# Gated DeltaNet layer on one core: the planner's periods replaced by five chains

## The chip, the cores and the metric

One core of one Trainium2 chip. The metric is device microseconds (us) of one execution of the whole program, the median of several runs. Engines are called as in the profile: PE (matmul; PEld is its weight load), DVE, ACT, POOL, SP (which issues DMAs). Each engine runs its own list of instructions in order and waits on semaphores for the others.

## The reference, cut to what matters

One layer (DEPTH = 1), so the attention mixer of the reference is never reached. x is 1024 x 1024.

```python
h    = rms_norm(x) * (1 + scale(c)) + shift(c)
proj = h @ w_in                      # 8 heads of q, of k; 16 of v, of z; b, a
qkv  = silu(causal_conv4(qkv))       # depthwise, 4 taps
q, k = l2norm(q) * 128**-0.5, l2norm(k)
beta, g = sigmoid(b), -exp(a_log) * softplus(a + dt_bias); gc = cumsum(g) by chunk of 64
decay = exp(where(lower, gc[c] - gc[s], -inf))
t    = inverse(I + strict_lower(beta k k^T * decay))
# scan over chunks
v_new = t(beta v) - t(beta k exp(gc)) @ state
o     = (q exp(gc)) @ state + (q k^T * decay) @ v_new
state = state * exp(gc_last) + (k exp(gc_last - gc))^T @ v_new
out   = rms_norm(x + gate(c) * ((rms_norm(o) * silu(z)) @ w_out))
```

## The kernel before

**Numbers.** All is f32. The large products run as three fp32r matmuls: every factor is split into a high half (`whi`, written by ACT, L586) and a low half (`wlo`, written by POOL, L587), and hi*hi, hi*lo and lo*hi are added in PSUM. A "tile" is 128 output columns of `w_in` against all 1024 tokens: 2 halves of 24 matmuls of 512 columns (`project`, L598).

**Groups.** The 16 v heads are worked on in 8 groups of two, with their common q and k head. For group gi:

- `proj_kq`: tiles of k and q, each with a convolution (`Conv`: ACT copies, three DVE operations L557, a Silu on ACT L561).
- `norms`: loads the decay exponents `em` (128 x 2048), 16 DVE additions (L641), one Exp on ACT (L644); k and q are transposed on PE (L659, L667) and their norms taken.
- `stage_a`: per chunk a product of k with k and q (L704), DVE makes `at` from it (L706); then by DRAM to another layout, 31 steps of substitution on DVE (L733, L736, one after the other), back by DRAM, and two calls of `levels` (L766 to L800), which build the inverse `TT` of each half of the tokens on PE, DVE and ACT.
- `values`: two v tiles with convolution, then a turn on PE (L813).
- `out_gate`: one z tile; its Silu (L868) is stored to DRAM.
- `scan`: 8 steps, each ks (L940), r on DVE (L943), ts (L963), vd on DVE (L967), vh and o on ACT (L969, L975), oq (L973, and in `second` L910), state (L982, L987). `second` of a step is issued in the next one. Outputs that are ready wait in a list `late`; `finish` turns one (L892), scales it (L896) and multiplies it by z (L897).

`residual_gate` makes the layer's gate (DVE at lowest rank), `early_loads` and `early` begin the output projection (L1067) with 4 of its 16 heads as soon as the projections are over.

**Who sets the order.** Between 78 us and about 1000 us the order on every engine is written out by a planner that runs while the kernel is built. Each stage is a generator; it issues a PE instruction and advances a clock `order.now`, puts other engines' operations into queues with an estimated cost, and yields a condition. An operation starts in the model when its inputs are ready (`LAT` after them, and no earlier than `now + LAT` of its issue); among operations that are ready on an engine the lowest `rank` goes first. `done` is true `LATP` after the modelled end. `drive` steps, at each turn, the first stage in its list whose condition holds. The chip then runs these orders with semaphores: where the model was wrong, an engine stands at the head of its list and waits.

`drive` is called once per **period** gi = -1 .. 7, and returns when all stages of that period are over:

```python
streams.append(scan(gi, Gs[gi]))
streams.append(stage_a(gi + 1, Gs[gi + 1], ...))
more = proj_kq(gi + 2, Gs[gi + 2], ...)
filler = [zfill, values(gi + 1, Gs[gi + 1], more)]
must = [Run(g) for g in streams] + [Run(itertools.chain(*filler))]
drive(background + must + ([zruns[gi + 2]] if ...) + [trun] * (gi >= HQ - 2), must)
```

So a period holds the scan of one group, `stage_a` (with `norms` in it) of the next and the k and q tiles of the one after; the z tiles of the following period (`zruns[gi + 2]`) can be taken early. In groups 0 and 7 the second `levels` call stands beside the scan (`LEV1`). The output projection's other 12 heads follow outside the planner.

## Time and profile before

| | |
|---|---|
| median of 3 runs | 1152.65 us (1149.68 to 1159.56) |
| profiled execution | 1154.56 us, its span 1152.8 us |
| granted TensorE clock, mean | 0.97 |
| busy: PE, PEld, DVE, ACT, POOL | 1075.8, 859.8, 757.8, 542.7, 440.1 us |

The span is first to last instruction. A matmul's row lasts longer than the step to the next one, since matmuls are pipelined; so PE's busy time is no measure of its work, but the time in which PE is *not* busy is time in which nothing flowed through it. Idle time stands before an instruction with what ended it.

### The profile page before, as it was taken

To read this page: it belongs to the slowest core of one execution; us is meant where nothing else is said; L and a number is where in the kernel's file an instruction comes from. 1 tells how busy PE (TensorE), PEld (TensorE's weight loads), DVE (VectorE), ACT (ScalarE), POOL (GpSimd) and SP (SyncE) were. 2 spreads that over 40 slices of the span, in tenths; PEclk is the share of its full clock that TensorE was granted. 3 is DMA by queue.
4 is the path that set the end of the run, shared out by engine and by line. 5 is a ranking of instruction groups with operands and counts; after the bars stand their busy time and mean duration, and the time that the engine had idled before them with its cause. 6 is when DMAs were issued, how large, how long until landed. Compare 5 with 4: busy or idle time off the path is not lost.

```text
span 1152.8 us, 18300 instructions
## 1 busy us (share of the span) xinstructions
PE 1075.8 (93%) x6295; PEld 859.8 (75%) x6295; DVE 757.8 (66%) x1913; ACT 542.7 (47%) x1415; POOL 440.1 (38%) x530
## 2 busy tenths in 40 slices
PE   7999998989999999899989998999999889999997
PEld 7877786867787777677867786778787657788785
DVE  5458963697789757776686678577767766413514
ACT  6457921443662346336623743374356424424523
POOL 3351321352352115313622452154215234844643
PEclk9899997999999889999999999999999979999999
DMA  9812142233154322421423052215212474335441
GB/s 286 224 37 91 42 119 69 69 102 95 40 150 120 84 78 67 122 69 47 119 61 110 27 148 56 75 39 144 65 56 70 115 231 134 101 114 182 153 128 73
DMA packets 187555, 118.43 MB, mean 103 GB/s; under 512 B 59669, under 2 KB 166470, under 8 KB 186438
## 3 DMA queue, kind: packets, MB, share of 16 engines
q1 hardware_dynamic: 186960, 117.15, 35.7%
q8 instruction: 50, 0.82, 0.3%
q14 instruction: 43, 0.35, 0.1%
q10 hardware_dynamic: 502, 0.10, 0.0%
HBM read 91.98 MB, written 25.24 MB: 102 GB/s over the span
## 4 chain that ended last, share of the span: by engine, by line
PE 43%; DVE 23%; ACT 11%; DMA 8%; issue 6%; POOL 6%; SPq 2%; DVEq 0%; ACTq 0%; POOLq 0%
PE pj L598 20%; DVE tm L733 5%; DVE tb L736 5%; PE pj L1067 4%; DVE vT L557 3%; DMA ua<-D 2%; DVE em L641 2%; DMA woraw<-in_gdn_w_out 2%; POOL wolo L206 2%; PE tr L704 2%; PE tr L797 2%; PE tr L789 2%; ACT tr L662 1%; ACT tr L669 1%; DVE kq L557 1%
## 5 line engine op out<-in xcount | busy, mean ns | idle before, releaser
L587 POOL TENSOR_TENSOR wlo<-wraw,whi 128x512 fp32r<-128x512 f32 x88 | 120.1, 1380 | 301.0 <-ACT whi L586 291.3
L733 DVE TENSOR_TENSOR tm<-tb,ua 128x126 f32<-128x126 f32 (+22 forms) x248 | 81.2, 327 | 25.3 <-DMA ua<-D 18.9
L557 DVE SCALAR_TENSOR_TENSOR kq<-xb,taps,kq 128x512 f32<-128x512 f32 x96 | 76.4, 804 | 22.3 <-ACT kq L554 19.2
L736 DVE TENSOR_TENSOR tb<-tb,tm 128x126 f32<-128x126 f32 (+22 forms) x248 | 82.2, 331 | 6.9
L557 DVE SCALAR_TENSOR_TENSOR vT<-xb,taps,vT 128x512 f32<-128x512 f32 x96 | 82.1, 855 | 5.0 <-ACT vT L554 3.9
L598 PE MATMUL pj<-h0hia,whi 128*128 128x512 f32 x184 | 77.6, 422 | 1.3 <-ACT kq L554 1.3
L598 PE MATMUL pj<-h0loa,whi 128*128 128x512 f32 x184 | 78.6, 427 | 0.0
L598 PE MATMUL pj<-h1lob,whi 128*128 128x512 f32 x184 | 77.4, 421 | 0.0
L598 PE MATMUL pj<-h0hia,wlo 128*128 128x512 f32 x184 | 77.2, 419 | 0.0
L598 PE MATMUL pj<-h0lob,whi 128*128 128x512 f32 x184 | 76.7, 417 | 0.0
L598 PE MATMUL pj<-h1loa,whi 128*128 128x512 f32 x184 | 76.3, 414 | 0.0
L598 PE MATMUL pj<-h1hia,wlo 128*128 128x512 f32 x184 | 76.2, 414 | 0.0
L598 PE MATMUL pj<-h0hib,wlo 128*128 128x512 f32 x184 | 76.0, 413 | 0.0
L598 PE MATMUL pj<-h1hia,whi 128*128 128x512 f32 x184 | 75.3, 409 | 0.0
L598 PE MATMUL pj<-h1hib,whi 128*128 128x512 f32 x184 | 75.3, 409 | 0.0
L598 PE MATMUL pj<-h0hib,whi 128*128 128x512 f32 x184 | 74.7, 406 | 0.0
L598 PE MATMUL pj<-h1hib,wlo 128*128 128x512 f32 x184 | 74.6, 405 | 0.0
L922 POOL TENSOR_TENSOR sso<-sso,neg_half 128x2 f32<-128x2 f32 x64 | 45.6, 713 | 71.4 <-DVE sso L920 67.9
L552 ACT COPY xb<-pj 128x512 f32<-128x512 f32 x62 | 36.1, 582 | 67.4 <-PE pj L598 63.7
L897 POOL TENSOR_TENSOR oT<-oT,z 128x256 f32<-128x256 f32 x64 | 48.1, 751 | 51.7 <-ACT oT L896 44.9
L896 ACT ACTIVATE oT<-pot,cols 128x256 f32<-128x256 f32 x64 | 30.3, 474 | 78.5 <-PE pot L892 76.8
L206 POOL TENSOR_TENSOR wolo<-woraw,wohi 128x512 fp32r<-128x512 f32 x36 | 48.7, 1371 | 44.7 <-ACT wohi L205 44.7
(459 smaller groups left out, 2923.6 us busy)
## 6 DMA issues: line engine op xcount, KB each, us to landing
wraw<-in_gdn_w_in SPq DMA_DIRECT2D x92, 256.0 KB, 3.3
woraw<-in_gdn_w_out SPq DMA_DIRECT2D x50, 256.0 KB, 3.2
wa<-in_ada_w SPq DMA_DIRECT2D x16, 512.0 KB, 7.0
em<-gc_dram SPq DMA_DIRECT2D x8, 1024.0 KB, 5.3
z_dram<-sz SPq DMA_DIRECT2D x32, 256.0 KB, 2.1
z<-z_dram SPq DMA_DIRECT2D x64, 128.0 KB, 2.4
o_dram<-oT SPq DMA_DIRECT2D x64, 128.0 KB, 1.9
gsrc<-o_dram SPq DMA_DIRECT2D x32, 256.0 KB, 3.0
```

The source lines that it names most:

```text
L206: nc.gpsimd.tensor_tensor(lo, raw, hi.bitcast(F32), op=ALU.subtract)
L552: a = act(lambda: nc.scalar.copy(xb[:, NTAP - 1:], ps), 512, *old, rank=0, holds=held)
L557: d = [vec(lambda j=j: nc.vector.scalar_tensor_tensor(dst, xb[:, j:j + TH], tp[:, j], dst, op0=ALU.mult, op1=ALU.add), 512, *d)]
L587: ops.append(pool(lambda raw=raw, ks=ks, hi=hi, lo=lo: nc.gpsimd.tensor_tensor(lo[:, ks], raw, hi[:, ks].bitcast(F32), op=ALU.subtract), 1 ...
L598: nc.tensor.matmul(ps, lhsT=a[:, k], rhs=b[half][k // 4][:, k % 4], start=(k == 0 and n == 0), stop=(k == KT - 1 and n == 2))
L641: e = [vec(lambda n=n, h=h: nc.vector.scalar_tensor_tensor(em[:, h, n], em[:, h, n], ngc[:, n, h0 + h:h0 + h + 1], mask, op0=ALU.add, op1= ...
L733: d = [vec(lambda j=j, mm=mm, ln=ln, tmv=tmv: nc.vector.tensor_tensor(tmv, tb[:, :mm, j:j + 1].to_broadcast([P, mm, ln]), ua[:, j:j + 1, j ...
L736: d = [vec(lambda j=j, mm=mm, tmv=tmv: nc.vector.tensor_tensor(tb[:, :mm, j + 1:], tb[:, :mm, j + 1:], tmv, op=ALU.subtract), 220 + mm * l ...
L896: a = act(lambda: nc.scalar.mul(oT, pot, normw_c), 470, holds=held)
L897: b = pool(lambda: nc.gpsimd.tensor_tensor(oT, oT, z, op=ALU.mult), 800, a, zo)
L922: d = pool(lambda: nc.gpsimd.tensor_tensor(sso, sso, neg_half[:, :2], op=ALU.pow), 700, d)
L1067: nc.tensor.matmul(acc, lhsT=a[:, ts], rhs=b, start=(first and n == 0), stop=(last and n == 2))
```

## The change

- The periods go. `drive` is called once, with five chains that each run over all 8 groups: scans; `outputs` (the former `finish`, now a stage of its own, with `late` and the fetched z tiles shared by all groups); `stage_a`, with both `levels` calls in it for every group; `norms`, one group after the other; and one chain of projections in the order values(0), z, values(1), k and q of 2, z, values(2), and so on. Beside them run the loader, the gate, and the early part of the output projection.
- What the periods had kept apart is now kept by conditions: buffers `kq`, `vtok`, `TT`, `em` wait for the scans that read them (`passed`, `gone`). `order.lock` and `LEV1` go.
- The PSUM bank `oq` is counted: a step of the scan is not issued before the planner thinks its readers done (`free("oq")`).
- The Exp over `em` is issued as four pieces of 128 x 512, at rank 2.
- `wlo` on POOL gets rank 2 and cost 1400 (was 1290).
- An operation is taken to start no earlier than `now + 380` after its issue (`LATE`; was 200), `LATP` is 300 (was 320).

```diff
-LATS, LAT, LATP, DMA = 50, 200, 320, 2800
+LATS, LAT, LATP, LATE = 50, 200, 300, 380
...
-        op = Op(eng, cost, fn, [a for a in after if a is not None], rank, table, self.now + LAT)
+        op = Op(eng, cost, fn, [a for a in after if a is not None], rank, table, self.now + LATE)
...
-                    lo[:, ks], raw, hi[:, ks].bitcast(F32), op=ALU.subtract), 1290, a, holds=r))
+                    lo[:, ks], raw, hi[:, ks].bitcast(F32), op=ALU.subtract), 1400, a, rank=2, holds=r))
...
+                    yield lambda: not old or done(old.passed[hf])
                     G.kq.append(cp.tile([P, 2, TH], F32, name="kq", tag="kq", bufs=4))
...
-        yield lambda: hasattr(order, "gate") and done(*order.gate, order.gc)
+        yield lambda: hasattr(order, "gate") and done(*order.gate, order.gc) and (gi < 2 or Gs[gi - 2].gone())
...
-        G.emop = act(lambda: nc.scalar.activation(em, em, AF.Exp), 1820, *e, table="exp")
+        G.emop = [[act(lambda x=em[:, h, n:n + 4]: nc.scalar.activation(x, x, AF.Exp), 512, *e[2 * n:2 * n + 8], rank=2,
+                       table="exp") for h in range(2)] for n in range(0, NT, 4)]
...
-        yield from levels(gi, G, 0, old)
-        if gi not in LEV1:
-            yield from levels(gi, G, 1, old)
+        yield from levels(gi, G, 0)
+        yield from levels(gi, G, 1)
...
-        yield lambda: not order.lock and (not (hf and old) or done(old.passed[0]))
-        order.lock = True
+        yield lambda: 2 * gi + hf < 3 or done(Gs[gi - 2 + hf].passed[1 - hf])
...
+                        yield lambda: 2 * gi + hf < 3 or done(Gs[gi - 2 + hf].passed[1 - hf])
                         G.vtok.append(cp.tile([P, 4, 2, P], F32, name="vtok", tag="vtok", bufs=3))
...
-                d = vec(lambda: nc.vector.tensor_tensor(o, o, po[:, 1], op=ALU.add), 256, *oo)
+                d = vec(lambda: nc.vector.tensor_tensor(o, o, po[:, 1], op=ALU.add), 256, *oo, holds=held)
...
-            yield lambda: hf in G.TTop and done(*ro, G.TTop[hf], G.nop[hf][4], *G.emop2)
+            yield lambda: hf in G.TTop and done(*ro, G.TTop[hf], G.nop[hf][4], *G.emop2) and free("oq")
             TT = G.TT[hf]
-            po = bank("oq", (P, 2, 2, P))
+            po, held = bank("oq", (P, 2, 2, P)), order.hold("oq", 3 if n else 1)
...
+        scans = Run(chain(scan(gi, G) for gi, G in enumerate(Gs)))
+        finishing, last = Run(outputs()), Run(early())
+        drive([Run(loader()), Run(early_loads()), Run(streams0), scans, finishing,
+               Run(chain(stage_a(gi, G) for gi, G in enumerate(Gs))), Run(chain(norms(gi, G) for gi, G in enumerate(Gs))),
+               Run(residual_gate()),
+               Run(chain([proj_kq(1, Gs[1])] + [values(gi, G, chain(others(gi))) for gi, G in enumerate(Gs)])), last],
+              [scans, finishing, last])
```

`others(gi)` yields `proj_kq(gi + 1)` (for gi > 0), then the z tiles: 5 after group 0, then 2, and 1 before the last.

## Rows read from the trace of the kernel before

**Rows 1.** The page: busy time and instructions of each engine.

```profile
PE 1075.8 (93%) x6295; PEld 859.8 (75%) x6295; DVE 757.8 (66%) x1913; ACT 542.7 (47%) x1415; POOL 440.1 (38%) x530
```

**Rows 2.** Windows by stage: start:end, length, busy us of each engine, PEclk, DMA.

```profile
76.00:181.00 105.00, 100.40 (x457) 80.00 (x456) 80.66 (x208) 61.42 (x143) 27.91 (x32) 1.00 0.24 74
181.00:202.00 21.00, 16.83 (x122) 12.55 (x121) 4.72 (x11) 2.70 (x5) 2.50 (x2) 0.61 0.33 78
202.00:297.00 95.00, 89.57 (x663) 71.22 (x663) 72.54 (x179) 39.27 (x108) 32.44 (x45) 1.00 0.33 88
297.00:421.00 124.00, 116.04 (x692) 91.57 (x690) 100.38 (x285) 57.15 (x157) 42.08 (x53) 0.96 0.36 98
...
638.00:747.00 109.00, 103.04 (x653) 82.48 (x652) 78.52 (x204) 53.92 (x153) 39.37 (x51) 1.00 0.30 81
...
919.00:961.00 42.00, 34.09 (x194) 24.00 (x193) 27.15 (x55) 10.92 (x19) 14.80 (x11) 0.80 0.61 191
961.00:1010.00 49.00, 47.07 (x321) 38.69 (x320) 26.83 (x65) 24.62 (x82) 34.27 (x41) 1.00 0.41 124
```

**Rows 3.** The same view, one window from 76 us to 1010 us.

```profile
76.00:1010.00 934.00, 873.83 (x5327) 694.93 (x5326) 670.23 (x1758) 448.14 (x1244) 335.84 (x427) 0.97 0.32 90
```

**Rows 4.** Windows with the projections' matmuls alone (L598): PE, PEld, PEclk, DMA.

```profile
638.00:747.00 109.00, 76.97 (x288) 52.70 (x288) 1.00 0.30 81
```

**Rows 5.** Chain that ended last, 266 to 273 us: start, us, what.

```profile
266.28 5.60 PE pj L598 x24
```

**Rows 6.** Waits of PE: who waited for whom, us in total, times, longest.

```profile
PE tr L813 <- ACT vT L561: 16.1, 11, 2.9
PE oq L973 <- DVE o L913: 7.7, 6, 1.6
PE ks L982 <- DVE vd L967: 6.9, 13, 1.1
...
PE tr L766 <- DVE TE L758: 3.5, 1, 3.5
PE ts L963 <- DVE r L943: 2.9, 6, 1.7
...
PE tr L778 <- ACT pn L772: 1.4, 1, 1.4
...
PE tr L789 <- DVE TE L782: 1.2, 1, 1.2
```

**Rows 7.** Timeline, all engines, 549 to 553 us: start, us, what, idle before.

```profile
547.89 1.28 ACT L644 ACT_TABLE_LOAD   x1
...
549.18 1.91 ACT L644 ACTIVATE em<-em 128x2048 f32<-128x2048 f32 x1
...
551.00 0.61 ACT L975 ACTIVATE o<-oq,eall 128x128 f32<-128x128 f32 x2
...
551.64 0.42 DVE L913 TENSOR_TENSOR o<-o,oq 128x256 f32<-128x256 f32 x1 [0.28 <-ACT o L975]
...
552.21 0.67 PE L973 MATMUL oq<-st,kq 128*128 128x256 f32 x2 [1.31 <-DVE o L913]
```

**Rows 8.** Timeline of DVE, then of PE, around 580 to 594 us.

```profile
581.32 0.30 DVE L733 TENSOR_TENSOR tm<-tb,ua 128x133 f32<-128x133 f32 x1
581.65 1.29 DVE L736 TENSOR_TENSOR tb<-tb,tm 128x133 f32<-128x133 f32 x1
...
589.98 0.74 DVE L557 SCALAR_TENSOR_TENSOR vT<-xb,taps,vT 128x512 f32<-128x512 f32 x1
...
593.11 0.66 PE L813 MATMUL tr<-ident,vT 128*128 128x128 f32 x4 [2.81 <-ACT vT L561]
```

**Rows 9.** Timeline: group 7's last k/q tile, first L704, first scan step.

```profile
856.53 0.69 ACT L554 ACTIVATE kq<-pj,taps 128x512 f32<-128x512 f32 x1
...
879.89 1.03 PE L704 MATMUL tr<-kq 128*128 128x256 f32 x4
...
960.87 0.61 PE L963 MATMUL ts<-vtok,TT 128*128 128x128 f32 x4
```

More of the change, by code (lines that the diff above doesn't have):

```diff
@@ L616, in __init__, with gone, proj_kq @@
             self.vop, self.ats, self.inverted = {}, None, [False, False]
-            self.nop, self.TTop = [], {}
-    def proj_kq(gi, G, old):
+            self.nop, self.TTop, self.normed, self.left = [], {}, False, None
+        def gone(self):
+            return self.left is not None and all(o.end is not None for o in self.left)
+    def proj_kq(gi, G):
         G.kq = []
+        old = Gs[gi - 2] if gi > 1 else None
         for j, ct in ((0, 8 + gi), (1, gi)):
@@ L868, in out_gate, with fetch @@
             load(store, act(lambda ps=ps, sz=sz: nc.scalar.activation(sz, ps, AF.Silu), 512, rank=0, table="silu",
-                            holds=ph))
+                            holds=ph), holds=held)
             yield None
+    late, zs = [], {}
+    def fetch():
+        for G, gi, n, *_ in late:
+            if (gi, n) not in zs and len(zs) < ZB and G.gated[n // 4] == 2:
+                z = cp.tile([P, 2, P], F32, name="z", tag="z", bufs=ZB)
+                zs[gi, n] = z, load(lambda z=z, n=n, h=2 * gi: nc.sync.dma_start(
+                    out=z, in_=z_dram[h:h + 2, :, n * P:(n + 1) * P].rearrange("h e t -> e h t")))
@@ new lines, in finish @@
+    def finish():
+        G, gi, n, o, op = late.pop(0)
+        pot, held = bank("pot", (P, 2, P)), order.hold("pot", 1)
+        for h in range(2):
+            nc.tensor.transpose(pot[:, h], o[:, h], ident)
+        order.now += M2
+        oT, stored = cp.tile([P, 2, P], F32, name="oT", tag="oT", bufs=OB), order.hold("oT", 1)
+        z, zo = zs.pop((gi, n))
+        a = act(lambda: nc.scalar.mul(oT, pot, normw_c), 470, holds=held)
+        b = pool(lambda: nc.gpsimd.tensor_tensor(oT, oT, z, op=ALU.mult), 800, a, zo)
+        load(lambda: nc.sync.dma_start(
+            out=o_dram[2 * gi:2 * gi + 2, :, n * P:(n + 1) * P].rearrange("h e t -> e h t"), in_=oT), b, holds=stored)
@@ L888, in finish @@
-        def finish():
-            n, o, op = late.pop(0)
-            pot, held = bank("pot", (P, 2, P)), order.hold("pot", 1)
-            for h in range(2):
-                nc.tensor.transpose(pot[:, h], o[:, h], ident)
-            order.now += M2
-            oT, stored = cp.tile([P, 2, P], F32, name="oT", tag="oT", bufs=OB), order.hold("oT", 1)
-            z, zo = zs.pop(n)
-            a = act(lambda: nc.scalar.mul(oT, pot, normw_c), 470, holds=held)
-            b = pool(lambda: nc.gpsimd.tensor_tensor(oT, oT, z, op=ALU.mult), 800, a, zo)
-            load(lambda: nc.sync.dma_start(
-                out=o_dram[h0:h0 + 2, :, n * P:(n + 1) * P].rearrange("h e t -> e h t"), in_=oT), b, holds=stored)
-            fetch()
@@ L902, in can_finish, with second @@
-        def can_finish():
-            fetch()
-            return late and late[0][0] in zs and done(late[0][2]) and free("pot") and order.avail("oT", OB)
-        def second(n, po, vh, vo, o, oo):
+        def second(n, po, vh, vo, o, oo, held):
             hf, j = divmod(n, 4)
@@ L946, in scan @@
                 second(*pend)
-                if len(late) > 2 and can_finish():
-                    finish()
                 if n < NT - 1:
@@ L988, in scan @@
                               rank=-1)
-            pend = (n, po, vh, vo, o, oo)
+            pend = (n, po, vh, vo, o, oo, held)
             yield lambda: done(*vo)
         second(*pend)
-        while late:
-            yield can_finish
-            finish()
+        G.left = [op for q in order.queue.values() for op in q]
+        yield None
     never = Op()
     def residual_gate():
+        yield lambda: Gs[RG - 1].left is not None
         gate_c = const.tile([P, KT], F32, name="gate_c")
@@ L1207, in drive @@
                 assert idle < 20000, [r.gen for r in must if not r.over]
-    def follow(run):
-        while not run.over:
-            yield lambda: run.over or not run.wait or run.wait()
-            run.step()
     order.projecting, order.early0 = True, False
```

100 lines of the change are left out of this document (35 added, 65 removed).

## The prediction, made before the changed kernel was run

> **What bounds the kernel now.** I read the page first: PE is busy for 1075.8 of 1152.8 us and no other engine is over 66% [rows 1]. PE's busy time overstates work, so I went on with what is left over: the time in which PE is not busy, stage by stage [rows 2], and over the whole stretch that the planner orders, 76 to 1010 us, in one row [rows 3]. The reader should see two things there. PE idles 934.0 - 873.8 = 60 us, and its clock is 0.97 of full speed on average, which is at most 0.03 x 934 = 28 us more. All other 846 us are matmuls that the change neither adds nor removes. So the most that any new order can win is 60 + 28 = 88 us, and this needs a perfect one.
>
> Next question: does PE idle because the periods leave it without work? I looked at a middle period, 638 to 747 us. It is 109 us long and PE is busy for 103.0 of it at full clock [rows 2]; it runs 288 projection matmuls, which is exactly the six tiles (two each of z, v and k/q, 48 matmuls each) that a period owes [rows 4]. A tile's half goes through in 5.60 us for 24, 233 ns each [rows 5], so projections take 288 x 0.233 = 67 us and the scan, products, turns and levels the rest. A join of periods would show as a hole of many us at 638 or 747; the whole period has 6 us, in pieces. So in the middle the joins cost next to nothing directly: z tiles of the next period fill them.
>
> What the idle time is made of stands in the table of PE's waits [rows 6]. Its longest single wait is 3.5 us. These are waits at the head of PE's list: the planner believed an operand finished that was not. The two largest kinds, with a picture each:
>
> - PE waits for DVE to empty the bank oq: 7.7 us in six waits. One of them in time order [rows 7]: the table load and the big Exp hold ACT for 1.28 + 1.91 us; the two small ACT operations on o start only at 551.00; DVE's addition follows at 551.64; then PE may write the bank, 1.31 us late.
> - PE waits for the Silu of vT before its turn: 16.1 us in eleven waits. DVE was in the substitution, one of whose operations had just taken 1.29 us in place of 0.30, and the convolution of vT began only at 589.98; the turn came 2.8 us late although other projections could have run [rows 8].
>
> At both ends it is worse: 181 to 202 us has 4.2 us idle and a clock of 0.61, 919 to 961 us has 7.9 us idle and a clock of 0.80 [rows 2].
>
> **The change part by part**, as PE time saved (-) or lost (+). The sum is made against the profiled execution, 1154.56 us (span 1152.8 and 1.8 around it), which is 1.9 us above the median of 1152.65.
>
> 1. *oq counted, Exp in pieces.* Both act on the same 7.7 us [rows 6], so they count once. The planner now issues other matmuls while the bank is read, and ACT is held for 1.28 us and a quarter of 1.91 at a time. The scan's step gets a longer modelled wait (its ts now also waits for the addition of the step before), which projections behind it in the filler chain cover; without that cover it would be about 0.4 us (L913's duration [rows 7]) x 8 steps x 8 groups = 26 us. Between -7.7 and 0: I take -7.
>
> 2. *Start of operations 180 ns later in the model, `done` 20 ns earlier.* Every hop PE to DVE or ACT to PE is modelled 160 ns longer. That acts on waits for vd and r, 6.9 + 2.9 us in 19 waits [rows 6], on average 0.52 us each. 19 x 0.16 = 3. Bounds -9.8 to 0: -3. On the vT waits likewise 11 x 0.16 = 1.8: -2, bounds -16 to 0.
>
> 3. *No periods.* In the middle 0 directly, as shown. Indirectly it parts work that used to crowd: `norms` and the em additions of a group no longer start together with the scan. What this does to one group [rows 9]: from the last k/q tile (856.53) to its first product L704 (879.89) 23 us pass, in which the decay table was loaded, added and exponentiated; with `norms` ahead only a Silu and the norms remain, by my estimate some 4 us. The first scan step then is due about 20 us sooner than the 104 us after that tile. But the time sooner is worth little as long as PE has projections to run, which it has until 919 us. At the end it moves the scan of group 7 towards 940 us, into a stretch that idles because the first output weights and rows are being loaded and split [rows 2]. Bounds -14 (idle and clock there, 7.9 + 0.2 x 42 = 16, less what the loads keep) to +8 (early products crowding the scan): -4.
>
> 4. *The start.* Group 0's chain to its first levels call ends in a wait of 3.5 us for a DRAM round trip [rows 6], and then 0.39 x 21 = 8 us go in clock [rows 2]. The Exp in pieces lets the first half of group 0 begin a little earlier; the round trip stays. But stage_a(1) now starts after levels(0, 1) in place of beside it, by my estimate half of that 21 us window later. Bounds -12 to +10: -2.
>
> 5. *Group 2's levels*, 297 to 421 us: waits of 1.4 and 1.2 us [rows 6] and 0.04 x 124 = 5 us of clock [rows 2], because DVE also made the gate there (100.4 us busy). The gate runs beside other work again. Bounds -7 to 0: -3.
>
> 6. *Costs.* ACT gets 24 more Exp instructions and up to three more pairs of table loads per group, 8 x 6 x 1.28 = 62 us at most, about a third of that if the pieces of a half stay together. ACT is busy for 448 of 934 us [rows 3]; it costs nothing but where a load stands before a step of the scan, as above [rows 7]. +1.5, bounds 0 to +10. `wlo` at rank 2 lets scan operations go first on POOL (336 of 934 us); behind a late low half stand 24 matmuls, but weights are made a tile ahead: 0, bounds -3 to +3.
>
> Sum: -7 - 3 - 2 - 4 - 2 - 3 + 1.5 = -19.5, so 1135 us for the profiled execution and 1133 against the median. I forecast **1133 us**.
>
> On item 6 the Trainium skill speaks against this change: "ScalarE: Activation LUTs", section "What ACT_TABLE_LOAD costs", puts a switch at 1.28 us of load and 1.38 us of drain, and "Table sets: the hidden batching unit" has all calls of a set batched, not interleaved. Here the load agrees at 1.28 us, but the Exp begins 20 ns after the load has ended [rows 7], so a drain shows at most before it. By the page's 2.66 us item 6 would be 8 x 6 x 2.66 = 128 us of ACT at most and about +3 in the sum, 1134.5 us.
>
> **The rivals.**
>
> *A. The waits only move (no change, about 1150).* PE's idle time comes from DVE and ACT being later than modelled, not from periods. For it: the waits for vT keep their cause, DVE in the substitution, and a PE that is released in one place arrives sooner at the next late operand. Then only some of item 1 stays: -4, 1150. Against it: oq was plainly not in the model, now it is.
>
> *B. The ends come in as well (about 1105).* If the clock stays up at the start, in group 2 and at the end (8 + 5 + 8 = 21 us) and their idle time halves (another 8), on top of the forecast: 1133 - 29 = 1104. For it: all these lie next to a stage that waited for one chain alone, and the chains now run ahead of each other. Against: the round trips by DRAM and the loads after the projections are as long as before.
>
> *C. DVE falls behind (slower, about 1178).* Place: the substitution. When POOL makes a low half, a DVE operation beside it takes 1.29 us in place of 0.30 [rows 8], which no cost in the model holds; there are 12 such halves per group. In a period DVE was busy for 78.5 of 109 us [rows 2], and a stretch of em additions and scan came before each substitution, in which it caught up. If em additions, products and convolutions now lie within it, it does not, and everything that PE takes from DVE comes late. Price: two turns and two scan steps per group later by 1.3 to 2.8 us, 8 x 4 x 1.4 = 45 us on top of the forecast. It decides from the point at which DVE has no idle time left over some 40 us of substitution.
>
> *D. The split Exp does harm (about 1165).* Every added table load stands before a step of the scan and costs as much as the one shown [rows 7]: up to 24 x 1.31 = 31 us on top. This is the rule of "ScalarE: Activation LUTs" (the Trainium skill), "Table sets: the hidden batching unit", in this kernel's numbers. Against: at rank 2 the pieces go when nothing else is ready.
>
> **How the numbers follow.** The forecast (1121 to 1141) gets 0.48, A 0.22, B 0.16, C 0.10, D 0.04. One per cent is 11.5 us, about what runs of this kernel can tell from no change (they span 1149.7 to 1159.6): faster means below 1141, slower above 1164. Faster: 0.46 of the forecast, all of B and a little of A, 0.64. Same: the rest of A and the forecast's edge, 0.23. Slower: C and most of D, 0.13. The range for 8 in 10 takes in the lower bounds of the unknown costs (those of items 1, 2 and 5 alone give 1152.7 - 7.7 - 9.8 - 16 - 7 = 1112) and most of B on one side, down to 1099, and A with its spread on the other, up to 1157; what lies outside is C, D and the far end of B.
>
> **What would show it.** Right: PE's waits L973 on DVE near 0; waits for vd and r about two thirds of 9.8 us; L704 of group 7 about 5 us after its last k/q tile; PE idle from 76 us to the end of the scans near 45 us, where it was 60; table loads before Exp 8 to 24. A shows as the same 60 us under other names. C shows as vT waits well over 16 us, with DVE above 23 of 25 us in the substitution; D as L973 or L910 waiting on ACT behind L644. My forecast fails if the joins cost something that rows of idle time don't show, such as matmuls run at half clock or pieces of PE work spaced by the model itself, or if the start or the end depends on the order of chains more than items 3 and 4 allow.

## The result, and the profile after

The changed kernel takes 1146.39 us (median of 9 runs, 1144.58 to 1149.82), the kernel before 1154.12 us (9 runs). The ratio is 0.9935, with a 95% interval of 0.9914 to 0.9957: a gain of about 8 us where 19.5 were forecast. The time lies inside the range, but nearer to rival A than to the forecast. Engine totals of the profiled execution (1145.48 us, span 1143.8):

```profile
PE 1067.9 (93%) x6295; PEld 862.2 (75%) x6295; DVE 745.7 (65%) x1913; ACT 563.6 (49%) x1451; POOL 444.7 (39%) x530
```

PE's idle time, span less busy time, is 1143.8 - 1067.9 = 75.9 us; before it was 1152.8 - 1075.8 = 77.0 [rows 1]. It hardly fell. From 76 us to the end of the scans it is 924.0 - 865.7 = 58.3 us, where 60 stood before and the prediction looked for about 45. So nearly all of the gain lies in time in which PE counts as busy: 1067.9 us in place of 1075.8, for the same 6295 matmuls. The waits of PE, 76 to 1010 us, in total, times, longest:

```profile
PE tr L816 <- ACT vT L561: 27.2, 9, 6.4
PE ks L987 <- DVE vd L972: 3.7, 4, 1.2
...
PE tr L783 <- ACT pn L777: 1.9, 1, 1.9
...
PE tr L771 <- DVE TE L763: 1.3, 1, 1.3
...
PE ts L968 <- DVE r L951: 0.7, 1, 0.7
...
PE oq L921 <- ACT o L980: 0.6, 2, 0.4
```

Set this beside [rows 6]. The bank's row, 7.7 us, is gone. vd and r fell from 9.8 to 4.4 us, and TE (DVE's transpositions at the start of the levels) from 3.5 to 1.3. One large row rose: turns (transpositions on PE) that wait for vT, from 16.1 us (longest 2.9) to 27.2 us (longest 6.4), in fewer waits. One of the long waits on the timeline, all engines (start, us, what, idle before):

```profile
553.28 0.19 DVE L740 TENSOR_TENSOR tm<-tb,ua 128x31 f32<-128x31 f32 x1 [3.07 <-DMA ua<-D]
...
556.39 2.65 POOL L587 TENSOR_TENSOR wlo<-wraw,whi 128x512 fp32r<-128x512 f32 x2 [11.89 <-ACT whi L586]
...
556.66 1.24 DVE L743 TENSOR_TENSOR tb<-tb,tm 128x100 f32<-128x100 f32 x1
...
557.93 1.23 DVE L740 TENSOR_TENSOR tm<-tb,ua 128x96 f32<-128x96 f32 x1
...
559.19 0.26 DVE L743 TENSOR_TENSOR tb<-tb,tm 128x96 f32<-128x96 f32 x1
...
559.99 2.69 POOL L587 TENSOR_TENSOR wlo<-wraw,whi 128x512 fp32r<-128x512 f32 x2 [0.95 <-ACT whi L586]
...
560.11 1.30 DVE L740 TENSOR_TENSOR tm<-tb,ua 128x110 f32<-128x110 f32 x1
...
561.45 1.36 DVE L743 TENSOR_TENSOR tb<-tb,tm 128x110 f32<-128x110 f32 x1
...
563.75 0.70 ACT L554 ACTIVATE vT<-pj,taps 128x512 f32<-128x512 f32 x1
...
572.29 0.74 DVE L557 SCALAR_TENSOR_TENSOR vT<-xb,taps,vT 128x512 f32<-128x512 f32 x1
...
574.70 0.63 ACT L561 ACTIVATE vT<-vT 128x512 f32<-128x512 f32 x1 [10.25 <-DVE vT L557]
...
575.38 1.12 PE L816 MATMUL tr<-ident,vT 128*128 128x128 f32 x4 [6.31 <-ACT vT L561]
```

DVE stands idle for 3.07 us before the substitution, because `ua`, the substitution's input, is not back from DRAM. Its load takes no longer than before (median from issue to landing 4.1 us, 4.0 before, 2.8 in the model), but DVE now waits for it longer, 35.8 us in all groups together in place of 18.9. The first of its two lines, before and after (count, busy us, mean ns, idle before):

```profile
L733 DVE TENSOR_TENSOR tm<-tb,ua 128x126 f32<-128x126 f32 (+22 forms) x248 | 81.2, 327 | 25.3 <-DMA ua<-D 18.9
...
L740 DVE TENSOR_TENSOR tm<-tb,ua 128x126 f32<-128x126 f32 (+22 forms) x248 | 81.2, 327 | 41.8 <-DMA ua<-D 35.8
```

Then four steps, one for each low half that POOL makes, take 1.23 to 1.36 us in place of some 0.27: 4 us more. So DVE is 7 us behind its written order. vT's convolution has its inputs at 564.5, but in DVE's list it stands behind steps that the planner thought over by then, and starts at 572.29. PE, with the turn at the head of its own list, idles 6.31 us. And the wait costs twice; windows (start:end, length, busy us of PE, PEld, DVE, ACT, POOL, granted clock, DMA):

```profile
287.00:386.00 99.00, 94.12 (x620) 74.84 (x619) 80.26 (x251) 51.53 (x142) 37.06 (x48) 1.00 0.39 106
...
553.00:578.00 25.00, 18.69 (x77) 14.60 (x76) 22.37 (x64) 10.65 (x17) 6.30 (x6) 0.92 0.23 64
...
574.00:581.00 7.00, 5.62 (x16) 4.61 (x17) 6.39 (x16) 2.72 (x5) 2.57 (x3) 0.52 0.00 0
601.00:710.00 109.00, 102.30 (x647) 83.26 (x646) 76.40 (x203) 56.62 (x157) 39.89 (x51) 0.97 0.30 81
792.00:799.00 7.00, 3.15 (x10) 2.67 (x11) 6.50 (x18) 2.72 (x5) 1.55 (x3) 0.52 0.00 0
903.00:947.00 44.00, 32.80 (x204) 23.80 (x203) 29.20 (x60) 10.90 (x19) 16.14 (x12) 0.88 0.57 180
947.00:1000.00 53.00, 50.56 (x307) 41.10 (x308) 28.66 (x63) 23.32 (x75) 30.80 (x37) 0.87 0.33 105
```

From 574 to 581, just behind the idle time, the granted clock is 0.52, the lower of its two levels (1.2 GHz); 0.51 stands at 683 and 0.52 at 792. A middle stretch of one group is as long as a period was, 109 us, and its clock is 0.97 where it was 1.00 [rows 2]. The end didn't improve either: 44.0 - 32.8 = 11.2 us idle between the last projection and the last scan (7.9 before), and then a clock of 0.87 (1.00 before). Group 2's stretch did: 4.9 us idle in 99 us at full clock, against 8.0 in 124 us at 0.96 [rows 2].

Table loads in front of Exp, from the groups by line (busy us, mean ns):

```profile
L650 ACT ACT_TABLE_LOAD x14 | 18.0, 1283 | 0.2
```

The landmarks of group 7, one line's instructions each (ns min/median/max, first and last start):

```profile
L561 ACT ACTIVATE kq<-kq x4: 631/632/640, 825.3 to 863.4; 128x512 f32<-128x512 f32 x4
...
L711 PE MATMUL tr<-kq x16: 378/379/483, 853.6 to 873.1; 128*128 128x256 f32 x16
...
L968 PE MATMUL ts<-vtok,TT x32: 272/275/377, 194.0 to 947.3; 128*128 128x128 f32 x32
```

The products of group 7 begin before its last k/q tile is through (853.6 against 863.4), for its first half needs only the first half's tiles. The last row is the first scan step of every group: group 0's at 194.0, group 7's at 947.3, where before the latter was at 960.87 [rows 9].

### The profile page after: what moved, and what is told of

Read it like the earlier page. It is cut to its first block, busy times and chain, and to the rows that moved or that the text cites. A ratio compares the mean times of both kernels' runs of the same rounds, so it can differ in the third digit from the quotient of the medians.

```text
span 1143.8 us, 18346 instructions
## 1 busy us (share of the span) xinstructions
PE 1067.9 (93%) x6295; PEld 862.2 (75%) x6295; DVE 745.7 (65%) x1913; ACT 563.6 (49%) x1451; POOL 444.7 (39%) x530
## 4 chain that ended last, share of the span: by engine, by line
PE 60%; DVE 18%; DMA 7%; ACT 5%; issue 3%; POOL 3%; SPq 3%; DVEq 0%; POOLq 0%; ACTq 0%
PE pj L598 25%; DVE tb L743 5%; DVE tm L740 5%; PE pj L1072 5%; DMA ua<-D 3%; PE tr L1072 2%; DVE vT L557 2%; PE tr L711 2%; PE ts L968 2%; PE oq L921 2%; PE ks L987 2%; PE ks L948 2%; PE tr L794 2%; PE oq L978 2%; PE tr L802 2%
## 5 line engine op out<-in xcount | busy, mean ns | idle before, releaser
L587 POOL TENSOR_TENSOR wlo<-wraw,whi 128x512 fp32r<-128x512 f32 x88 | 117.7, 1350 | 289.0 <-ACT whi L586 249.6
L740 DVE TENSOR_TENSOR tm<-tb,ua 128x126 f32<-128x126 f32 (+22 forms) x248 | 81.2, 327 | 41.8 <-DMA ua<-D 35.8
L743 DVE TENSOR_TENSOR tb<-tb,tm 128x126 f32<-128x126 f32 (+22 forms) x248 | 84.6, 341 | 6.8 <-DVE tm L740 0.3
L898 POOL TENSOR_TENSOR oT<-oT,z 128x256 f32<-128x256 f32 x64 | 53.5, 836 | 80.0 <-ACT oT L897 78.6
L598 PE MATMUL pj<-h0loa,whi 128*128 128x512 f32 x184 | 80.5, 438 | 0.0
L598 PE MATMUL pj<-h0hia,whi 128*128 128x512 f32 x184 | 78.4, 426 | 1.3 <-ACT kq L554 1.3
L598 PE MATMUL pj<-h0hia,wlo 128*128 128x512 f32 x184 | 78.5, 427 | 0.7 <-POOL wlo L587 0.7
L598 PE MATMUL pj<-h1loa,whi 128*128 128x512 f32 x184 | 77.4, 421 | 0.0
L598 PE MATMUL pj<-h1lob,whi 128*128 128x512 f32 x184 | 76.8, 418 | 0.0
L598 PE MATMUL pj<-h1hib,wlo 128*128 128x512 f32 x184 | 76.7, 417 | 0.0
L598 PE MATMUL pj<-h1hia,whi 128*128 128x512 f32 x184 | 76.4, 415 | 0.0
L598 PE MATMUL pj<-h1hib,whi 128*128 128x512 f32 x184 | 76.3, 414 | 0.0
L598 PE MATMUL pj<-h1hia,wlo 128*128 128x512 f32 x184 | 76.1, 414 | 0.0
L598 PE MATMUL pj<-h0hib,wlo 128*128 128x512 f32 x184 | 76.1, 414 | 0.0
L598 PE MATMUL pj<-h0hib,whi 128*128 128x512 f32 x184 | 75.6, 411 | 0.0
L598 PE MATMUL pj<-h0lob,whi 128*128 128x512 f32 x184 | 75.3, 409 | 0.0
L561 ACT ACTIVATE vT<-vT 128x512 f32<-128x512 f32 x32 | 20.2, 631 | 108.4 <-DVE vT L557 108.4
L586 ACT CAST whi<-wraw 128x512 fp32r<-128x512 f32 x88 | 52.4, 619 | 39.9 <-DMA wraw<-in_gdn_w_in 38.8
L974 ACT ACTIVATE vh<-ts,brk 128x128 f32<-128x128 f32 x128 | 43.4, 365 | 46.4 <-PE ts L968 23.9
```

What stands on the lines that cost most here:

```text
L586: a = act(lambda raw=raw, ks=ks, hi=hi: nc.scalar.copy(hi[:, ks], raw), 512, d, rank=2)
L587: ops.append(pool(lambda raw=raw, ks=ks, hi=hi, lo=lo: nc.gpsimd.tensor_tensor(lo[:, ks], raw, hi[:, ks].bitcast(F32), op=ALU.subtract), 1 ...
L598: nc.tensor.matmul(ps, lhsT=a[:, k], rhs=b[half][k // 4][:, k % 4], start=(k == 0 and n == 0), stop=(k == KT - 1 and n == 2))
L740: d = [vec(lambda j=j, mm=mm, ln=ln, tmv=tmv: nc.vector.tensor_tensor(tmv, tb[:, :mm, j:j + 1].to_broadcast([P, mm, ln]), ua[:, j:j + 1, j ...
L743: d = [vec(lambda j=j, mm=mm, tmv=tmv: nc.vector.tensor_tensor(tb[:, :mm, j + 1:], tb[:, :mm, j + 1:], tmv, op=ALU.subtract), 220 + mm * l ...
L898: b = pool(lambda: nc.gpsimd.tensor_tensor(oT, oT, z, op=ALU.mult), 800, a, zo)
```

## The experiments

Every run was timed beside the kernel before on the same chip. So the ratios to that kernel are what to compare; they stand here with the total of PE's waits for vT (us, 76 to 1010 us) of each.

| run | edit, in short | us | ratio (95%) | vT |
|---|---|---|---|---|
| changed kernel | | 1146.39 | 0.9935 (0.9914 to 0.9957) | 27.2 |
| e1_lo_memset | low half a memset | 1107.78 | 0.9627 (0.9588 to 0.9665) | 10.5 |
| e13_subst_260 | step cost 260 | 1117.48 | 0.9707 (0.967 to 0.9745) | 11.3 |
| e2_subst_cost | step cost 300 | 1108.32 | 0.9638 (0.9588 to 0.9687) | 3.7 |
| e3_ua_late | ua 1.5 us later in the model | 1132.39 | 0.984 (0.9788 to 0.9893) | 17.2 |
| e4_both | e2 and e3 | 1128.25 | 0.981 (0.9767 to 0.9854) | 4.8 |
| e9_oq_uncounted | bank not counted | 1162.3 | 1.0105 (1.0034 to 1.0176) | 20.5 |
| e10_late_back | old delays | 1146.68 | 0.9951 (0.9917 to 0.9985) | 20.8 |
| e8_one_exp | one Exp | 1139.74 | 0.991 (0.9881 to 0.9939) | 16.0 |
| e7_periods_rest | periods, all else changed | 1139.85 | 0.9909 (0.9872 to 0.9945) | 13.7 |
| e6_periods_lo_memset | kernel before, memset | 1105.11 | 0.9601 (0.9564 to 0.9637) | 2.4 |
| e5_periods_rest_subst | e7, step cost 300 | 1170.03 | 1.0162 (1.0125 to 1.02) | 1.0 |
| e11_subst_one_exp | e2 and e8 | 1160.01 | 1.0077 (1.0045 to 1.0108) | 7.2 |
| e12_low_on_dve_model | low half charged to DVE | 1158.75 | 1.0053 (1.0021 to 1.0086) | 3.9 |
| e14_one_exp_vtok4 | e11, fourth vtok | 1150.2 | 0.9995 (0.9962 to 1.0028) | 5.7 |
| e15_subst_vtok4 | e2, fourth vtok | 1124.08 | 0.9761 (0.9724 to 0.9798) | 5.3 |
| e16_subst_levels | e2, chain cut | 1114.3 | 0.9686 (0.9651 to 0.9722) | 4.1 |
| e17_one_exp_levels | e11, chain cut | 1124.17 | 0.9775 (0.9738 to 0.9812) | 7.2 |
| e18_chg_levels | changed kernel, chain cut | 1143.81 | 0.9918 (0.9889 to 0.9948) | 18.4 |

### Is it the substitution beside POOL, and the waits for vT?

**POOL's subtraction replaced, the order kept (e1_lo_memset).** The low halves are zeros; their share of the projections is left out.

```
-  ops.append(pool(lambda ...: nc.gpsimd.tensor_tensor(lo[:, ks], raw, hi[:, ks].bitcast(F32), op=ALU.subtract), 1400, a, rank=2, holds=r))
+  ops.append(pool(lambda ...: nc.gpsimd.memset(lo[:, ks].bitcast(F32), 0.0), 1400, a, rank=2, holds=r))
```

> The changed kernel in the same order, but POOL writes the low halves of w_in with a memset to zero in place of the subtraction: the share of the products that the low halves give is left out, and POOL reads nothing. Theory P (POOL's subtraction stretches DVE's substitution steps from 0.3 to 1.3 us, about four of them before each vT turn): no step over 0.4 us beside a low half any more, PE's waits for vT fall from 27.2 to under 9 us, the half-clock stretches of 6.8 us behind them (574, 683, 792 us) go, 1120 to 1132 us. Theory D (the substitution starts late because the load of ua lands after 4.1 us where 2.8 are modelled): the steps don't matter, vT waits stay above 18 us, 1140 us or more. Rival S (waits only shift): vT waits fall, others rise by as much, 1143 to 1148 us.

The order written by the planner is the same, as is every cost in it; the chip alone differs. 0.9627. Groups by line of the changed kernel, then of this run (count, busy us, mean ns, idle before):

```profile
L587 POOL TENSOR_TENSOR wlo<-wraw,whi 128x512 fp32r<-128x512 f32 x88 | 117.7, 1350 | 289.0 <-ACT whi L586 249.6 <-DVE gt L388 14.7 <-PE tr L773 14.0
...
L743 DVE TENSOR_TENSOR tb<-tb,tm 128x126 f32<-128x126 f32 (+22 forms) x248 | 84.6, 341 | 6.8 <-DVE tm L740 0.3
```

```profile
L587 POOL MEMSET wlo<- 128x512 f32 x88 | 44.5, 527 | 226.5 <-PE pj L598 226.4
...
L743 DVE TENSOR_TENSOR tb<-tb,tm 128x126 f32<-128x126 f32 (+22 forms) x248 | 66.7, 269 | 6.9 <-DVE tm L740 0.3
```

Its waits for vT:

```profile
PE tr L816 <- ACT vT L561: 10.5, 4, 3.0
```

The mean step falls from 341 to 269 ns, and the waits for vT from 27.2 to 10.5 us, not quite to the 9 expected; the time lies 12 us below the range expected, and lower clock is left behind two of the waits (at 551 and 660 us). DVE's busy time falls by 52.6 us in all (745.7 to 693.1), of which the two lines of the substitution are 31.3; so the run tests the subtraction's effect on all of DVE, and not on the substitution alone. The edit also frees POOL (117.7 to 44.5 us). PE's own waits for POOL in the ordered stretch are small and don't fall (5.1 us before the edit, 4.9 after), but what POOL's time does by way of other engines the run doesn't tell from the stretch.

**The model told of it (e2_subst_cost).** Nothing but two numbers of the planner:

```
-  ..., 220 + mm * ln // 2, *d, rank=2)]     # both operations of a substitution step
+  ..., 300 + mm * ln // 2, *d, rank=2)]
```

> The changed kernel, but the planner takes each of the 62 substitution steps to cost 80 ns more (300 + n/2 in place of 220 + n/2; 5 us per group). The chip does the same work in another order. Theory P, and D too: the planner no longer thinks vT done early, its turn is issued later, vT waits under 8 us, 1122 to 1134 us. Rival S: vT waits fall, the time stays at 1142 to 1150 us, because PE then waits for levels or scan.

0.9638, with POOL's subtractions all there. Waits, then the whole window:

```profile
PE ks L987 <- DVE vd L972: 5.2, 6, 1.6
...
PE tr L816 <- ACT vT L561: 3.7, 9, 0.6
```

```profile
76.00:1010.00 934.00, 899.55 (x5524) 724.19 (x5523) 672.03 (x1772) 480.51 (x1302) 360.47 (x443) 0.99 0.34 97
```

The steps stretch as before (L743's mean is 371 ns in this run), but the turns are now issued when vT is there. The time lies 14 us below the range expected. In the changed kernel the same window reads PE 874.07 and clock 0.96. It is the fastest version of the whole computation found here.

**A value in between (e13_subst_260)**, 260 in both places, to tell a cause from a lucky order:

> The changed kernel with the planner's cost of a substitution step at 260 in place of 220 (half of the way to the 300 that gave 1108.32). If the waits for vT in front of the level turns are what that edit removed, half of the edit removes a part of them: 1120 to 1138 us, with 8 to 20 us of waits for vT where the change has 43 and the edit at 300 has 4. If 1108 was one lucky order among many, there is no reason for a value in between: the time is anywhere from 1105 to 1160, and waits for vT don't go with it.

220, 260, 300 give waits of 27.2, 11.3, 3.7 us and ratios of 0.9935, 0.9707, 0.9638: time and waits go together. The time lies 2.5 us below the range expected. (That text's 43 us for the change's waits is larger than the row's 27.2; the row holds.)

**The late DMA alone (e3_ua_late), and both (e4_both).** An empty operation of 1500 ns on SP's queue between ua and the first step:

```
+  d = [order.put("sp", 1500, lambda: None, d)]
```

> The changed kernel, but the planner takes the load of ua to land 1.5 us later than it did (4.3 in place of 2.8 us); nothing is added on the chip. Theory D: vT waits under 10 us, 1125 to 1135 us. Theory P: every long vT wait is shorter by about 1.5 us only, 27 to about 20 us in sum, 1140 to 1145 us. Rival S: no change in time.

> The two modelled costs of the runs before together: 80 ns more per substitution step, ua 1.5 us later. Theories P and D: vT waits under 4 us and no half-clock stretch behind them, 1118 to 1132 us. Rival S: 1142 to 1150 us.

0.984 and 0.981. Modelling the DMA later takes 10 of the 27 us of waits away, nearly as much as the change had added, and DVE's idle time for `ua` falls from 35.8 to 22.7 us; so both theories hold a part. Together with the step cost the waits are nearly all gone (4.8), but 20 us of e2's gain are lost again; the third group of runs below is about that.

### The other parts of the change

**The count of the bank taken out (e9_oq_uncounted)**: ` and free("oq")` removed from the condition ahead of ts.

> The changed kernel without the condition that the bank oq is free; all else as changed. As predicted (item 1): waits of PE for DVE's o before L978 come back, 5 to 8 us, 1150 to 1156 us. If the four Exp pieces alone had removed them: under 2 us of such waits and 1142 to 1149 us.

1.0105 against 0.9935, some 20 us, above the range expected. Waits:

```profile
PE oq L978 <- DVE o L924: 13.2, 8, 2.5
...
PE oq L978 <- DVE o L926: 2.8, 2, 2.0
```

The 16 us of waits that the count removes are there to be seen. In the new order it is worth about double what the old order's 7.7 us promised.

**The delays back (e10_late_back)**: `LATE` 200, `LATP` 320.

> The changed kernel with the modelled start at now + 200 and done at 320 ns again. As predicted (item 2): waits for vd and r rise from 4.4 us by 3 to 5 us, 1148 to 1154 us. Rival P2 (the later modelled start is also what moved the convolutions of vT behind more substitution steps): vT waits fall to about the 16 us of before and the time to 1136 to 1142 us.

0.9951 against 0.9935, intervals overlapping. With the old delays vd waits 2.7 us in place of 3.7, r 3.7 in place of 0.7, TE 5.8 in place of 1.3, vT 20.8 in place of 27.2. So the longer delays shorten the waits for r and TE, not those for vd, and lengthen those for vT; the time doesn't show either. So of the 5.4 us by which these two waits fell against the kernel before, 3.4 come without the delays. The time lies in neither range expected.

**One Exp of 2048 columns (e8_one_exp)**, kept behind the additions:

```
+  G.emop = [[act(lambda: nc.scalar.activation(em, em, AF.Exp), 1820, *e, table="exp")]] * 2
```

> The changed kernel with one Exp of 128 x 2048 at rank 1 again, everything else as changed. If the pieces cost by their 12 added table loads (15 us of ACT): 1136 to 1143 us. If they help by holding ACT for a shorter time: 1149 us or more, with waits for o or vh behind the Exp. As predicted, within 4 us of 1146 us.

0.991 against 0.9935: some 3 us for the pieces, which the intervals can't tell from none. Loads in front of the Exp, the convolutions' Silu and the Silu of z fall from 14, 10 and 7 to 7, 7 and 3. The waits for vT are 16.0 us here, no more than in the kernel before, and yet the time is nearly that of the changed kernel: TE waits 8.7 us in their place.

**Periods kept, with all the other parts (e7_periods_rest).** The kernel before with the count of oq, the delays, the Exp in pieces and the low half at rank 2.

> The kernel before with its periods, and all other parts of the change: oq counted, Exp in four pieces, 380 and 300 ns, low halves at rank 2 and cost 1400. Theory as predicted (joins cost nothing, gain comes from oq and latencies): the waits for oq are gone, 1138 to 1148 us, as fast as the changed kernel or faster. Rival J (the chains are what gains): 1150 us or more, slower than the changed kernel by over 4 us.

0.9909 against 0.9935 for the chains. At these costs the joins of the periods cost nothing that can be measured in the whole time, and the chains win nothing of their own. Here too the waits for vT don't rise (13.7 us), but those for vd do, from 6.9 to 12.3 us, in spite of the longer delays. **The kernel before with the memset (e6_periods_lo_memset)**, with the low halves' share left out as in e1:

> The kernel before, in its own order, with the low halves of w_in written by a memset to zero on POOL in place of the subtraction; what the low halves add to the products is left out. Theory P (POOL's subtraction beside DVE is what makes PE wait, with periods too): vT waits fall from 16.1 to under 6 us, 1130 to 1142 us. If periods and chains suffered from it alike, it would gain the 39 us that it gained with chains, 1110 to 1118 us. Rival J (the joins bound the kernel before): waits fall, but the time stays within 8 us of 1150.

0.9601, as much as e1's chains. Of its waits the bank's stand where they were, and vT's are 2.4 us (16.1 before); the time lies 5 us below the lower of the ranges expected:

```profile
PE oq L973 <- DVE o L913: 7.3, 6, 1.6
...
PE tr L813 <- ACT vT L561: 2.4, 4, 0.9
```

So POOL's subtraction costs 4.0% in the old order and 3.1% in the new one (0.9935 to 0.9627). The change did not bring it and did not raise its price, though it lengthened the waits for vT. Two more things follow from setting e6 beside e1. Without the subtraction the waits for vT still are 2.4 us in the old order and 10.5 in the new one, so 8 of the 11 us by which the change raised them aren't the subtraction's doing. And without it the two kernels are level, 0.9601 and 0.9627, so the subtraction alone isn't what kept the change from its forecast gain.

### Why dearer models sometimes lose: the chain of one group

**Three more orders whose waits for vT are gone, and which are slow.** e5_periods_rest_subst is e7 with the step cost at 300; e11_subst_one_exp is e2 with one Exp; e12_low_on_dve_model charges DVE 1 us in the model for every low half that POOL makes, by `order.put("dve", 1000, lambda: None, (a,), rank=0)`.

> The run before it (periods, all other parts), and 80 ns more modelled cost for each substitution step. With chains this correction gave 1108 us. Theory as predicted (joins cost nothing): 1105 to 1118 us. Rival J (with the costs right, the joins bound): vT waits under 6 us, but 1122 us or more.

> Chains, 80 ns more modelled cost per substitution step (which alone gave 1108 us), and one Exp. If the pieces cost 7 us by themselves, as 1140 against 1146 us suggested: 1098 to 1104 us. If that difference was the order of other things: 1105 to 1120 us.

> The changed kernel, where the planner also keeps DVE busy for 1.0 us for every low half that POOL makes (an entry in DVE's modelled queue that issues no instruction); the substitution's own cost stays. Theory P (the missing cost is POOL's on DVE): vT waits under 10 us, 1105 to 1130 us, like the run with dearer steps. If the gain of that run was a lucky order: vT waits fall, but the time stays over 1135 us.

All three lose to the kernel before. e5 came out as its rival J had it: waits for vT of 1.0 us, and 1170 us. So with the dearer step the periods are 5% slower than the chains (1.0162 against 0.9638), and e7's finding that the joins cost nothing holds, as far as one order each can tell, for the old step cost alone. e11 lies outside both of its ranges, and e12 where its text looks for a lucky order: vT's waits gone (3.9 us), the time over 1135. Against luck alone stands e13, whose value in between gave a time in between. Two stretches of e5 stand out, around the first scan steps of groups 6 and 7: at 843 to 869 us PE is busy for 19.1 of 26 us at a clock of 0.54, at 955 to 982 us for 13.5 of 27 at 0.56, with 8 and 0 projection matmuls and waits for TE of 5.8 and 10.2 us.

In e11 the first scan steps and group 5's additions, k/q Silus and products read (first and last start):

```profile
L967 PE MATMUL ts<-vtok,TT x32: 270/275/521, 198.2 to 970.1; 128*128 128x128 f32 x32
...
L647 DVE SCALAR_TENSOR_TENSOR em<-em,ngc,mask x16: 322/345/353, 632.7 to 639.2; 128x128 f32<-128x128 f32 x16
...
L561 ACT ACTIVATE kq<-kq x4: 632/632/634, 599.4 to 617.5; 128x512 f32<-128x512 f32 x4
...
L710 PE MATMUL tr<-kq x16: 377/379/454, 654.7 to 667.7; 128*128 128x256 f32 x16
```

and a window of the same run, columns as above:

```profile
852.00:879.00 27.00, 22.88 (x168) 18.60 (x169) 16.76 (x48) 10.54 (x26) 5.99 (x8) 0.50 0.04 11
```

Groups follow each other by (970.1 - 198.2) / 7 = 110 us. The k/q tiles of group 5 lie done at 618, and its products begin 37 us later: the additions to its decay table end only at 639.5, and its Exp at 641.4. In the changed kernel group 5's products begin at 634.3, before its last k/q Silu at 644.0. There PE's projections are late; here the chain of a group is: `norms` takes the next decay table only when the scan two groups back counts as gone, and `stage_a` the next group only when it is through with the levels of this one. The last line shows what happens when this leaves PE without projections: 27 us at the lower clock, with no projection matmul.

**A fourth buffer for v's tokens (e14, e15)**, so that projections of v need not wait for the scan's half just before:

```
-  yield lambda: 2 * gi + hf < 3 or done(Gs[gi - 2 + hf].passed[1 - hf])      # bufs=3
+  yield lambda: gi < 2 or done(Gs[gi - 2].passed[hf])                        # bufs=4
```

> The step cost at 300 and one exponential of 2048 columns (1160.01 us together) with a fourth buffer for v's tokens, so that a group's projections wait for the scans' half of two groups before in place of the half just before. If that run was slow because the projections were held behind the scans' half, and PE's turns then had no projections to fill them, the time falls to 1125 or less, and the half clock (85 us) to under 50. If it was slow because the chain of one group (gram, ua, substitution, ub, the levels) takes some 105 to 108 us by itself, nothing moves: 1152 to 1162.

> The step cost at 300 (1108.32 us) with a fourth buffer for v's tokens. If the held projections cost anything in that kernel too, 1095 to 1105; if its projections never wait for the half, 1105 to 1112. If the chain of a group is the bound, no change, 1108, or a few us worse by another order.

The slow order gains 10 us, in neither range expected, and stays at 109 us a group ((957.8 - 194.4) / 7); the fast one loses 16 us, more than its text allowed. The buffer isn't the main cause.

**The chain cut in two places (e16, e17, e18).** `levels` becomes a chain of its own, so that the next products start once the first half's levels are done, and a scan counts as gone when its own operations are, without the substitution steps (rank 2) in the queues:

```
-        yield from levels(gi, G, 0)
-        yield from levels(gi, G, 1)
+  Run(chain(levels(gi, G, hf) for gi, G in enumerate(Gs) for hf in range(NHALF)))
-  G.left = [op for q in order.queue.values() for op in q]
+  G.left = [op for q in order.queue.values() for op in q if op.rank < 2]
```

> The same two cuts on the slow order, step cost at 300 and one Exp (1160.01 us, first scan steps 108 us apart). If the chain of one group is its bound, the first scan steps come 95 to 103 us apart and the time is 1105 to 1140. If the chain is not, and the order is bad for other reasons, 1150 to 1165.

> The step cost at 300 (1108.32 us), with the chain of one group cut in two places: levels run as a chain of their own, so that the products of group n+1 start once the first half of group n's levels is done, and a scan counts as gone when its own operations are done, without the substitution steps queued behind them. If the chain of one group (some 97 to 100 us between first scan steps there) is the next bound, the spacing falls and the time is 1080 to 1103 us. If PE's own work is the bound there, 1105 to 1115.

> The same two cuts on the changed kernel with nothing else (1146.39 us). There the products wait for their k/q tiles and not for the group before, so the chain is not the bound: 1140 to 1152 us, with waits for vT still over 25 us in all. If the chain were the bound there as well, 1130 or less.

e17, the cut on the slow order, in the same two views:

```profile
L967 PE MATMUL ts<-vtok,TT x32: 270/275/421, 194.4 to 933.5; 128*128 128x128 f32 x32
```

```profile
852.00:879.00 27.00, 24.08 (x110) 19.18 (x109) 14.19 (x43) 7.41 (x13) 5.23 (x10) 1.00 0.36 103
```

1.0077 becomes 0.9775, and 105.6 us a group in place of 110. The second line is the same stretch of time but not the same work, for here it holds 99 projection matmuls; ahead of group 6's first scan step (799.7 us in this run), 780 to 812 us holds 79 of them at full clock. The time is in the range that the chain's theory gave; the mean spacing fell less than it said (95 to 103), because the last of the seven is 133 us. The two cuts were not tried apart. On e2 the cut gains nothing (0.9686 against 0.9638, as expected if PE's own work is the bound there) and on the changed kernel neither (0.9918 against 0.9935, vT still 18.4 us, of which 25 were expected): there the chain wasn't the bound. So in e5 and e12 the chain is the likely cause too, with 111 and 109 us a group (in e5 with the joins, which wait for it), but there it was not cut, so this is not shown.

## Why the prediction was wrong, point by point

**The step that failed** is the second half of item 2, "on the vT waits likewise 11 x 0.16 = 1.8: -2, bounds -16 to 0". It priced these waits as if PE were early by a constant, one hop's delay, and allowed no rise. They rose by 11.1 us, and each of the three long ones was followed by a stretch at the lower clock. Their cause is no hop but DVE's lag in the substitution, which grows with every stretched step and with the wait for `ua`, and is paid by whatever stands behind those steps in DVE's list. That the lag costs time is shown from two sides, by taking the stretch away (e1) and by letting the model know of it (e2, e13): 26 to 35 us below the changed kernel by the ratios. The rise itself is mostly `ua`'s: DVE's idle time for it went from 18.9 to 35.8 us, a later modelled landing (e3) takes 10 us off the waits again, and 8 of the 11 us stay when the subtraction is gone from both kernels.

It is not the only one. **Item 3's end** was sized -4, and the stretch between the last projections and the last scan became 6.5 us longer (table below). And e7 and e8, whose waits for vT don't rise, gain only some 10 us, for other waits take their place (vd 12.3 us in e7, TE 8.7 us in e8). A wait that is removed is not time that is won; the sum took it so.

**Rival C** had the place and the mechanism: waits of more than 16 us, from 1.2 us steps. Its condition, a DVE without idle time, and its price, 45 us, were wrong. DVE was busy for 22.4 of 25 us there, and stood idle for ua first; a fixed order needs no full engine to be late, only an operation behind a lag that the order doesn't know. That the subtraction costs 46 us in the old order (e6) is near its price of 45 by chance: C meant what the change would add.

**Item 1** was right: the bank's waits went from 7.7 us to none (0.6 at L921), and taking the count out brings back 16. **Item 2, vd and r**: -3 forecast, -5.4 in the rows, but not by the delays: 3.4 of it are there without them (e10), and with them and the periods (e7) vd waits longer than before. **Item 3**, the joins cost nothing in the middle: so it is in the whole time at these costs (e7), and not with a dearer step (e5). Its -4 at the end was wrong: idle time there is 3.3 us more, and the last scan runs at 0.87. **Item 4**, -2: the first scan step comes 7.8 us sooner (194.0 against 201.8), but between 76 and 202 us PE is busy for 117.7 us against 117.2, clock 0.93 against 0.94, so little or nothing. **Item 5**, -3: right in its idle time (-3.1 us) and too small in all, for the clock came back as well. **Item 6**, +1.5: 14 loads before Exp, within the 8 to 24 named, and more before the Silus; e8 puts the cost at some 3 us, not to be told from none. (The Exp in [rows 7] starts 10 ns behind its load's end, not 20.)

**The sum.** By the waits' rows, bank and vd/r gave 13 us, TE 2, vT took back 11, and idle time in all fell by 1.1 us. Where the 9 us of the span lie can be estimated by cutting both traces at points of equal work, every matmul counted at the median step of its kind to the next:

| stretch before, us | length, idle, clock | stretch after, us | length, idle, clock |
|---|---|---|---|
| 0 to 286 | 286.0, 21.5, 0.95 | 0 to 280 | 280.0, 19.6, 0.96 |
| 286 to 473 | 187.0, 12.6, 0.96 | 280 to 452.5 | 172.5, 5.7, 1.00 |
| 473 to 563 | 90.0, 5.5, 1.00 | 452.5 to 541.5 | 89.0, 4.1, 0.98 |
| 563 to 915 | 352.0, 18.0, 1.00 | 541.5 to 900 | 358.5, 22.5, 0.97 |
| 915 to 974 | 59.0, 8.5, 0.86 | 900 to 965.5 | 65.5, 13.1, 0.82 |

The changed kernel is some 21 us ahead when about half of the work is done, most of it won where item 5 stands, in idle time and clock. It loses 6.5 us in the stretch with the three long waits for vT, and 6.5 at the end. So a gain of the forecast's size was there and was lost again; that the time fell inside the range is the balance of a term that was too small and two of the wrong sign, and so luck. Busy time at full clock shrank too, though the prediction had all time but idle time and clock as fixed ("All other 846 us"). What shortened it no run here tells.

**Rival A** is what happened in size: nearly the same idle time, 58.3 us, under other names. It named the cause too, "DVE in the substitution", without seeing that the order would expose more of it. **Rivals B and D** did not come: the last stretch idles more than before, and the waits of the bank for ACT are 0.6 us in all.

**Left open**: e2's 1108 us is an order's time, and orders that differ by one small edit lie 5 to 50 us apart (e2 against e16, e15, e4 and e11), so a difference of a few us between two of them isn't the price of an edit. Why DVE waits longer for `ua` in the order of the chains, and why the end became longer, was not tested.

## What to carry to other kernels

Where an order is written out ahead from modelled costs, look for the operation whose measured duration is bimodal (0.27 or 1.3 us here) and for the load that lands later than modelled (4.1 us for 2.8), and for what stands behind them in an engine's list: the lag goes to consumers that the model calls ready, and no constant delay per hop covers it. Telling the model helps, but not in every order: the dearer step won 3.0% on the changed kernel (e2), and lost 2.5% with the periods (e5) and 1.7% with one Exp (e11). So try the cost in the order that is to use it, and watch the distance between groups: when a dearer model makes the serial chain of one group longer than PE's own work, the filler runs out, and the clock goes with it.

## What the runs showed of the hardware

A DVE operation with two operands in SBUF that begins beside POOL's two-operand subtraction (1.35 us each) takes 1.23 to 1.36 us in place of 0.27; of the 496 operations of the substitution, counted in the traces, 25 took over 0.9 us before, 35 after, and 4 in e1, where POOL writes a memset of 0.53 us; 31 of the 35 overlap a subtraction, and none of the 4 a memset of a low half. The Trainium skill, "SBUF — State Buffer", section "SBUF: two separate sides", says that the two engines share one pair of ports as an exclusive lock, held for a whole instruction, and that a DVE operation with two SBUF inputs is concerned only against a GpSimd operation that reads SBUF; the traces agree in both, the stretch of a step by about one subtraction's time and its absence beside the memset. Its price here was 3.1 to 4.0% of a kernel in which DVE is busy for two thirds of the time.

PE's granted clock fell to its lower level for some 7 us behind each of the three waits of about 6 us (574, 683, 792 us in the changed kernel). Behind waits of just under 3 us it did not fall in some places (593 and 702 us in the kernel before, 2.8 us each) and did in others (811 us there, 2.9 us; 551 us in e1, 2.9 us). In e11 it stayed at the lower level for 27 us of scan steps and levels without projections (0.50).
